# A decoder step on one core: the MLP's second product in seven quarter products for eight

## The chip, the cores and the metric

The kernel runs on one core of a Trainium2 chip. The metric is the device time of one execution in microseconds (us). Three runs of the kernel before took 3097.52, 3102.01 and 3103.74 us; their median, 3102.01 us, is the time that the change is measured against.

## The reference, cut to what matters

One step of a decoder layer on 2048 prompt tokens and 32 sample tokens, in float32. A state-space mixer and a retention mixer come first, then an output projection, an attention over 256 memory tokens, a squared-ReLU MLP and a last normalisation. What the change touches is the MLP:

```
h = rmsnorm(x, p['g_mlp'])                                   # 1024 wide
x = x + jnp.square(jax.nn.relu(h @ p['w_up'])) @ p['w_down']  # 1024 -> 4096 -> 1024
```

## The kernel before

Everything is kept transposed: features on the 128 partitions, tokens along the free axis. A float32 matrix is split into two parts in a 32-bit format that TensorE multiplies fast (float32r): a high part, written by ScalarE as a copy, and a low part, the difference of the number and its high part, written by VectorE (DVE) or GpSimd (POOL). A product is then three passes, high by high, high by low and low by high (PASSES), all summed in one PSUM bank. `mm` (line 445 in the profile) issues each matrix instruction; each loads its own 128 by 128 weight tile (PEld) and streams the tokens past it (PE). All instructions of DVE, ScalarE (ACT), POOL and of the DMA queue on SyncE (SP) go through one helper, line 197, so they are told apart by the names of their tiles.

The tokens are cut into four blocks of 512 columns, numbered 1 to 4 here (0 to 3 in the code). After both mixers have run for all blocks, `rest_items` takes block after block through memory attention and MLP. The sample tokens come into the attention queries with block 2, have their own attention over caches during block 2's MLP (`sample_items`, 48 weight units put between the others, their sums held in one PSUM bank, `zps`), and go through the MLP with block 3, which therefore has 544 columns, taken as two pieces of 272.

Weights come in units of 128 by 1024 numbers (512 KB). `load_unit` (line 413) issues one DMA into `raw` (three buffers), `split_unit` (line 423) makes `whl` of it (high and low part, three buffers): the high part by an ACT copy, the low part by a subtraction on DVE or POOL. Two units are split ahead of the one in use, two more are loaded ahead.

The MLP (`mlp_items`, line 2102) works in eight groups g of 512 hidden features. `up_items(g)` takes four units of `w_up`; each gives one hidden tile of 128 features in 24 matmuls of 512 columns. Each tile then takes a scaled ReLU on DVE from PSUM (`relu`), a square on ACT as high part (`actl`), a square on DVE or POOL (`sq`) and the subtraction of both as low part (`actl`, eight buffers). `down_items(g)` (line 2135) takes four units of `w_down`; each serves two of the eight output tiles, by four hidden tiles, by three passes: again 24 matmuls of 512 columns. At the end of each output tile DVE adds the PSUM bank to the residual `x` (`add_to`, "x<-dn,x"). Order: up(0), up(1), down(0), up(2), down(1), and so on; "dn" in the names of a down matmul is the PSUM tile from `dense` (four banks in turn), "actl" its moving operand. In block 4 the last group's down product runs over the first 256 columns and then over the other 256, and the final normalisation (`final`, line 2186) of the first half starts while the second half is still being multiplied:

```
parts = [(0, BT // 2), (BT // 2, BT)] if g == 7 and B["last"] else [(0, t)]
```

The order of the program is made while it is built. `Order.run` emits the units one after the other, in the order of TensorE's time; chains (`Side`) such as normalisations are resumed when a small model of the engines' rates says that their operands are ready (`poll`). `Either` (line 201) gives an instruction to DVE or to POOL, whichever the model has done with it first, where its key in SET is 2; a weight unit whose engine is None is placed in the same way. Each engine then works through its own instructions strictly in that order.

Of the kernel before, what the change touches and what calls it, by code (L numbers as in the profile page):

```python
# [39 lines left out]
PASSES = ((0, 0), (0, 1), (1, 0))  # L40
GAMMA = [1.0 - 2.0 ** (-5.0 - h) for h in range(HEADS)]
# [16 lines left out]


class Item:  # L60
    """A piece of the main sequence: a weight unit to load and what to do with it, or a call."""
# [13 lines left out]
class Model:  # L75
    """Guesses when each engine does what it is given, from the operands and the engines' rates."""
# [11 lines left out]
    def where(self, ap):  # L88
        """First and last partition and element, outermost stride, elements within it."""
# [93 lines left out]
class Engine:  # L183
    """An engine whose instructions the model sees."""
# [16 lines left out]
class Either:  # L201
    """An instruction for the engine that SET names, or for the one that the model has done with it first."""
# [28 lines left out]
class Order:  # L231
    """Emits the program in the order of the tensor engine's time: a main sequence of weight units,
    and chains that come in between when their latencies have passed."""
# [5 lines left out]
    def spawn(self, gen, *aps):  # L239
        """A chain, from when the tiles are ready."""  # L240
        s = Side(gen, max(self.clock, self.model.ready(*aps)))
        self.sides.append(s)
        return s

    def resume(self, s):
        """A chain goes on when the engines have done what it gave them, or some time later, or when tiles are ready."""
# [15 lines left out]
    def work(self, out, ins, cost):  # L262
        """A matrix product."""
        self.clock = max(self.clock, self.model.after("PE", [out], ins)) + cost
        self.model.note("PE", [out], ins, self.clock)
# [63 lines left out]
def tile_decoder_step(ctx: ExitStack, tc: tile.TileContext, ins: dict, outs: dict):  # L329
# [56 lines left out]
    wo_d = dram.tile([HEADS, 2, P, 1024], F32, tag="wo_d", name="wo_d")  # L386

# [25 lines left out]
    def load_unit(src, into=None):  # L413
        raw = into() if into else wpool.tile([P, 1024], F32, tag="raw", name="raw", bufs=3)
        if isinstance(src, (list, tuple)):
# [7 lines left out]
    def split_unit(raw, eng, pool=None, tag="whl", bufs=NW):  # L423
        """Both float32r parts of a unit, [P, 2, 1024]."""
# [10 lines left out]
    def mm(out, lhsT, rhs, start, stop):  # L435
# [9 lines left out]
        T.matmul(out, lhsT, rhs, start=start, stop=stop)  # L445
# [15 lines left out]
    def split(dst, src, scale=None):  # L461
        """dst[:, 0] + dst[:, 1] = src (* scale) in float32r parts."""
# [3 lines left out]
    def rsqrt(pool, tag, x, n):  # L466
        """x ** -0.5 on [P, n]."""
# [15 lines left out]
    def fm(w, acts, t, out, nk=KT, order=None):  # L483
        """One 128-row tile of W^T X: w(k, s) gives lhsT; fills out with (PSUM tile, column, columns)."""
# [10 lines left out]
    def stats(pool, acc, cols, eps_tag):  # L495
        """(mean square + eps) ** -0.5 by token; cols: list of (lhsT slice of acc, rows, further summands)."""
# [21 lines left out]
    def spread(dst, rs, t, last=None, row=None):  # L518
        """dst[p, token] = rs[token]: rs column i holds tokens i*128.., `last` the sample column; row: space for 512 tokens."""
# [24 lines left out]
    def s5_setup(sp):  # L544
        """The tables and matrices of the state space, four pairs of groups at a time, into DRAM."""
# [27 lines left out]
        def turns(*gens):  # L573
            """One instruction of each in turn."""
# [9 lines left out]
        def poly(x, cs, out):  # L584
            """((cs[0] x + cs[1]) x + ...) x, without a constant term."""
# [123 lines left out]
        # a = mag (cos + i sin), and the parts of a product with it  # L709
# [63 lines left out]
        def products(out, n, x, y, tab, neg):  # L773
            """out gets the real and imaginary parts of (x + i y) tab, the latter with neg for tab."""
# [52 lines left out]
    def all_tables(jt, fhf, fl, hpi):  # L827
        """cos and sin of the angles' multiples."""
# [23 lines left out]
    # The sample tokens go with block SB up to the queries, then through the MLP with the next one.  # L852
# [23 lines left out]
    def fill(side, lst, n):  # L876
        """Runs a chain until lst has n entries."""
        while len(lst) < n and not side.done:
            od.resume(side)

    def fm_item(src, view, acts, t, done, nk=KT, eng=None, order=None, tag="lo"):
        """One weight unit: view(hl) gives a list of w(k, s); done(i, out) takes the i-th result."""
# [54 lines left out]
    def mem_items():  # L937
        """Keys and values of the memory, and the query and output weights with them multiplied in."""
# [105 lines left out]
    def mix_take(B, k, x, rest=None):  # L1044
        """One row tile of the input: its parts and squares; `rest` comes in between."""
# [54 lines left out]
    def first_load(B, units, side):  # L1100
        """The first block's input with the weights of its first product, and a chain in between."""
# [425 lines left out]
    def ret_keep(B, h, i, x):  # L1527
        """Sets the sample columns of a query, key or gate tile aside."""
# [172 lines left out]
    def squares(B, o, t, lo=0):  # L1701
# [10 lines left out]
        else:  # L1712
            sq = rk((P, TM_), "relu", 2) if "rest" in pool else xin()
            A.activation(sq[:, c], x[:, c], AF.Square)
            E("x_rq").tensor_tensor(out=B["acc"][:, c], in0=B["acc"][:, c], in1=sq[:, c], op=ALU.add)
# [11 lines left out]
    def normed_split(B, o, gain, hs, t):  # L1727
        """Its first part; gives what does the second."""
# [161 lines left out]
    def sample_keep(B):  # L1890
        """Sets the sample columns of the normalised input aside."""
# [7 lines left out]
    def sample_items():  # L1899
        """The sample tokens' queries, their attention over the caches, and its output weights."""  # L1900
# [48 lines left out]
    def sample_rows(Z):  # L1949
        """The sum of both parts of the rows in PSUM, and its transpose, tile by tile."""  # L1950
# [93 lines left out]
    def mo_last(B, u, ahead):  # L2044
        """The last two heads, row tile by row tile."""
# [56 lines left out]
    def mlp_items(B, nxt):  # L2102
# [58 lines left out]
        def mixed(items):  # L2161
            for i in items:
                yield i
# [209 lines left out]
```

## Time and profile before

| | |
|---|---|
| median of three runs | 3102.01 us |
| span of the profiled execution | 3086.3 us |
| PE busy | 2950.1 us, 96% |
| DVE, POOL, ACT busy | 1826.7, 1189.3, 1005.9 us |
| mean granted TensorE clock | 0.987 |
| moved by DMA | 374.32 MB |

The profiled execution spans 3086.3 us from its first to its last instruction; the median of the three timed runs lies 15.7 us above that. A duration in the profile is that of one instruction; matrix instructions overlap, so that their pace is read from when they start, not from how long one takes. "[0.85 <-ACT whl L197]" behind a row says that the engine was idle for 0.85 us before it and what ended the idle time. A granted clock of 1.00 is the higher of TensorE's two levels (2.4 GHz).

### The profile page before, as it was taken

How to read it: one execution, taken by the hardware profiler on the slowest of the kernel's cores; microseconds unless marked ns; L12 is line 12 of the kernel's file. 1: busy time of each engine (PE TensorE's matmuls, PEld its weight loads, DVE VectorE, ACT ScalarE, POOL GpSimd, SP SyncE). 2: the span in 40 equal slices, each digit the busy share in tenths (PEclk: the TensorE clock that was granted, in tenths of full speed). 3: DMA queues.
4: the chain of work that ended last, by engine and by line, in shares of the span. 5: the costliest groups of instructions: out<-in, count | busy, mean ns of one | idle time of the engine just before them, and what ended most of it. 6: DMA issues, size and time to landing. Idle time of an engine off the chain costs nothing.

```text
span 3086.3 us, 42360 instructions
## 1 busy us (share of the span) xinstructions
PE 2950.1 (96%) x16676; PEld 2566.3 (83%) x16676; DVE 1826.7 (59%) x3079; ACT 1005.9 (33%) x1440; POOL 1189.3 (39%) x764
## 2 busy tenths in 40 slices
PE   8898899998989999999999999999999999999998
PEld 6788787877877878887987888788999998878887
DVE  9968868679686563334465555655533344554334
ACT  4432232322444332223343333343322223332222
POOL 5424434244454243333524333361523325153333
PEclk9999999999999999999999999999999999999999
DMA  5452252342674322224324444542222233222222
GB/s 150 136 176 97 97 166 96 130 145 72 220 251 157 105 89 96 96 96 140 117 83 138 142 146 147 190 145 89 83 89 89 86 133 119 89 89 96 96 96 75
DMA packets 138950, 374.32 MB, mean 121 GB/s; under 512 B 18656, under 2 KB 39808, under 8 KB 138752
## 3 DMA queue, kind: packets, MB, share of 16 engines
q1 hardware_dynamic: 138176, 371.10, 36.1%
q8 instruction: 131, 2.15, 0.3%
q14 instruction: 67, 0.55, 0.1%
q10 hardware_dynamic: 576, 0.52, 0.1%
HBM read 334.17 MB, written 37.40 MB: 120 GB/s over the span
## 4 chain that ended last, share of the span: by engine, by line
PE 61%; DVE 2%; issue 1%; DMA 1%; ACT 1%; POOL 1%; SPq 0%; POOLq 0%; ACTq 0%; DVEq 0%
PE dn L445 54%; PE sc L445 6%; PE zps L445 1%; DMA raw<-in_w_down 1%; DVE rst L197 1%; ACT whl L197 0%; PE ptp L449 0%; DVE rsy L197 0%; DVE act L197 0%; DVE pmk L197 0%; PE st L445 0%; DVE whl L197 0%; POOL whl L197 0%; POOL act L197 0%; PE sp L445 0%
## 5 line engine op out<-in xcount | busy, mean ns | idle before, releaser
L445 PE MATMUL dn<-act,whl 128*128 128x512 f32 (+2 forms) x4704 | 914.2, 348 | 8.4 <-DVE whl L197 7.4
L445 PE MATMUL dn<-actl,whl 128*128 128x512 f32 (+2 forms) x4656 | 917.3, 356 | 5.1 <-DVE x L197 4.9
L445 PEld LDWEIGHTS dn<-actl,whl 128*128 128x128 f32 x4656 | 767.5, 188 | 134.6 <-issue 3.8
L445 PEld LDWEIGHTS dn<-act,whl 128*128 128x128 f32 x4704 | 753.4, 190 | 116.5 <-DVE whl L197 8.4
L197 POOL TENSOR_TENSOR whl<-raw,whl 128x1024 fp32r<-128x1024 f32 x225 | 559.1, 2487 | 549.1 <-ACT whl L197 536.1
L197 ACT ACTIVATE whl<-raw 128x1024 fp32r<-128x1024 f32 (+1 forms) x505 | 522.7, 1045 | 655.5 <-PE dn L445 445.2
L197 DVE TENSOR_TENSOR x<-dn,x 128x512 f32<-128x512 f32 (+2 forms) x496 | 291.1, 605 | 429.0 <-PE dn L445 428.3
L197 DVE TENSOR_TENSOR whl<-raw,whl 128x1024 fp32r<-128x1024 f32 (+1 forms) x280 | 401.7, 1441 | 165.2 <-ACT whl L197 152.9
L445 PE MATMUL dn<-z,whl 128*128 128x512 f32 (+1 forms) x2160 | 434.9, 353 | 0.0
L445 PEld LDWEIGHTS dn<-z,whl 128*128 128x128 f32 x2160 | 353.7, 188 | 56.8 <-issue 1.1
L197 POOL TENSOR_TENSOR actl<-sq,actl 128x512 fp32r<-128x512 f32 (+1 forms) x128 | 171.3, 1339 | 485.8 <-DVE sq L197 471.5
L197 DVE SCALAR_TENSOR_TENSOR relu<-dn,rb 128x512 f32<-128x512 f32 (+1 forms) x160 | 91.6, 589 | 324.7 <-PE dn L445 317.3
L197 ACT ACTIVATE actl<-relu 128x512 fp32r<-128x512 f32 (+1 forms) x128 | 82.0, 641 | 515.9 <-DVE relu L197 515.9
L445 PE MATMUL dn<-whl,act 128*128 128x512 f32 x768 | 200.1, 408 | 10.8 <-ACT whl L197 6.1
L197 POOL TENSOR_TENSOR acc<-acc,relu 128x512 f32<-128x512 f32 (+2 forms) x77 | 107.4, 1395 | 249.9 <-ACT relu L197 247.8
L445 PEld LDWEIGHTS dn<-whl,act 128*128 128x128 f32 x768 | 165.8, 253 | 34.4 <-ACT whl L197 6.8
L197 DVE TENSOR_TENSOR sq<-relu 128x512 f32<-128x512 f32 (+1 forms) x128 | 90.2, 704 | 14.8 <-POOL actl L197 2.3
L445 PE MATMUL sc<-whl,act 128*128 128x256 f32 x576 | 81.0, 293 | 15.0 <-ACT p L197 9.2
L445 PEld LDWEIGHTS sc<-whl,act 128*128 128x128 f32 x576 | 76.0, 200 | 16.1 <-ACT p L197 9.9
L197 DVE SCALAR_TENSOR_TENSOR act<-x,small,act 128x512 fp32r<-128x512 f32 (+2 forms) x76 | 70.0, 928 | 27.0 <-ACT act L197 26.9
L445 PE MATMUL sc<-whl,z 128*128 128x256 f32 x576 | 80.7, 291 | 0.0
L197 ACT ACTIVATE act<-x,small 128x512 fp32r<-128x512 f32 (+2 forms) x76 | 52.9, 699 | 78.9 <-DVE x L197 55.0
(317 smaller groups left out, 2743.9 us busy)
## 6 DMA issues: line engine op xcount, KB each, us to landing
raw<-in_w_up SPq DMA_DIRECT2D x128, 512.0 KB, 3.5
raw<-in_w_down SPq DMA_DIRECT2D x128, 512.0 KB, 3.5
raw<-in_w_out SPq DMA_DIRECT2D x32, 512.0 KB, 3.5
raw<-wq_d SPq DMA_DIRECT2D x32, 512.0 KB, 3.6
raw<-wo_d SPq DMA_DIRECT2D x32, 512.0 KB, 3.5
x<-in_xT SPq DMA_DIRECT2D x48, 256.0 KB, 4.3
pm<-pm_d SPq DMA_DIRECT2D x16, 768.0 KB, 4.6
tab<-tab_d SPq DMA_DIRECT2D x16, 516.0 KB, 3.5
```

Of the source, the lines that this page charges most:

```text
L197: return f(*args, **kw)
L445: T.matmul(out, lhsT, rhs, start=start, stop=stop)
```

## The change

In blocks 2 to 4 the down product of each group is done by Strassen's scheme in the form with few additions. For each group and each half u of the output tiles, the weights are seen as a 2 by 2 matrix of quarters, each 256 hidden features by 256 outputs, and the hidden tiles as a 2 by 2 matrix of quarters, each 256 features by half of the block's tokens. Seven products of quarters (JOBS) stand for eight; each has 12 matmuls of 256 columns (272 in block 3).

- The hidden squares are written to `hc` by DVE or POOL. A chain `hidden(g)` makes the four sums of them, and the two float32r parts of all seven operands: 4 subtractions, 7 ACT copies and 7 more subtractions, each on 2 by 256 columns. It goes on only as far as buffers of `actl` have been read.
- The sums of the weights' quarters, S1 to S4, don't depend on the block. `sums()` makes them while the first block is in its attention and MLP: 32 times a DMA of 512 KB in, four POOL subtractions or additions of 256 columns, a DMA of 512 KB out to `s_d`.
- `down_seven` pairs the 14 products of a group into seven weight units. A unit's halves come from the weights in a new layout (`w_s`) or from `s_d`, in one DMA, or in two of half the size when they don't lie beside each other.
- Partial sums stay in PSUM where they are needed again: A11, S2, S3 and A22 are added up in one bank, S1 and S4 in another, A12 has its own. After each product DVE adds the bank as it stands to the residual, two tiles of 256 columns, 28 such additions per group.
- In block 4 the last group isn't cut into halves of the columns any more, and the final normalisation runs once, over all 512 columns, behind the last product.
- `dynamic_dma_scratch_size` is made smaller.

```diff
+HQ = TM_ // 2
+JOBS = ("A11", "A12", "S2", "S1", "S3", "S4", "A22")
...
+    "l_ds": 4, "x_hs": 2, "x_hq": 2, "x_hl": 2, "q_h": 250, "ws": 700, "ws1": 1500, "ws2": 5000}
...
+    s_d = dram.tile([16, P, 4, 512], F32, tag="s_d", name="s_d")
...
+        src = src() if callable(src) else src
...
-            E("x_rq").tensor_tensor(out=B["acc"][:, c], in0=B["acc"][:, c], in1=sq[:, c], op=ALU.add)
+            (V if "tail" in B else E("x_rq")).tensor_tensor(out=B["acc"][:, c], in0=B["acc"][:, c], in1=sq[:, c], op=ALU.add)
...
-        def mixed(items):
-            for i in items:
+        def hidden(g, c):
+            h, ops = t // 2, a_of[g]
+            b11, b12, b21, b22 = (c[:, :, i, :h] for i in range(4))
+            def sub(out, a, b):
+                E("x_hs").tensor_tensor(out=out, in0=a, in1=b, op=ALU.subtract)
+            def keep(name, src):
+                before = divmod(7 * g + JOBS.index(name) - NL, 7)
+                while g and B["prog"] < 14 * before[0] + 8 + before[1]:
+                    yield 300
+                yield [src]
+                a = actl().rearrange("p a (s c) -> p a s c", s=2)
+                A.activation(a[:, :, 0, :h], src, AF.Copy)
+                yield [a]
+                E("x_hl").tensor_tensor(out=a[:, :, 1, :h], in0=src, in1=a[:, :, 0, :h].bitcast(F32), op=ALU.subtract)
+                ops[name] = a
+                yield SET["q_h"]
+            yield [c]
+            t2 = rk((P, 2, HQ), "t2")[:, :, :h]
+            yield from keep("A11", b11)
+            sub(b11, b12, b11)
+            sub(t2, b22, b11)
+            yield from keep("A12", b21)
+            sub(b21, b21, t2)
+            yield from keep("S2", t2)
+            sub(b12, b22, b12)
+            yield from keep("S1", b11)
+            yield from keep("S3", b12)
+            yield from keep("S4", b22)
+            yield from keep("A22", b21)
+        def up_seven(g):
+            a_of[g] = {}
+            c_of = {}
+            for m in range(4):
+                def done(_, out, m=m):
+                    def ev():
+                        if m == 0:
+                            c_of[0] = rk((P, 2, 4, HQ), "hc")
+                        c = c_of[0]
+                        r = rk((P, TM_), "relu", 2)
+                        for ps, lo, n in out:
+                            V.scalar_tensor_tensor(out=r[:, lo:lo + n], in0=ps[:, :n], scalar=0.0,
+                                                   in1=B["mrb"][:, lo:lo + n], op0=ALU.max, op1=ALU.mult)
+                        v = r[:, :t].rearrange("p (a b) -> p a b", a=2)
+                        E("x_hq").tensor_tensor(out=c[:, m // 2, 2 * (m % 2):2 * (m % 2) + 2, :t // 2], in0=v, in1=v, op=ALU.mult)
+                        if m == 3:
+                            hid[g] = od.spawn(hidden(g, c))
+                    if m == 0 and g:
+                        while not hid[g - 1].done:
+                            od.resume(hid[g - 1])
+                    ev() if "mrb" in B else pend.append(ev)
+                yield fm_item(ins["w_up"][4 * g + m], one, lambda: B["hm"], t, done, eng=ve("e_up1" if m % 2 else "e_up"), tag="l_up")
+        def seven(g, u, name, st):
+            h = t // 2
+            def job(w):
+                v = w.rearrange("p s (k m c) -> p s k m c", k=2, m=2)
+                while name not in a_of[g]:
+                    od.resume(hid[g])
+                for m in range(2):
+                    if name in ("A11", "S1"):
+                        st[name, m] = (aux2 if name == "S1" and not held["zps"] else dense)("m7")
+                    ps = st["S1" if name in ("S1", "S4") else "A11", m] if name != "A12" else aux("m7")
+                    for k in range(2):
+                        for i, (a, b) in enumerate(PASSES):
+                            mm(ps[:, :h], v[:, a, k, m, :], a_of[g][name][:, k, b, :h],
+                               start=(name in ("A11", "A12", "S1") and k + i == 0), stop=(k == 1 and i == 2), skip_group_check=True)
+                        yield
+                    o = 4 * u + m + (2 if name in ("A22", "S1", "S3") else 0)
+                    lo = h if name in ("S2", "S4", "S1", "S3") else 0
+                    V.tensor_tensor(out=B["x"][o][:, lo:lo + h], in0=ps[:, :h], in1=B["x"][o][:, lo:lo + h], op=ALU.add)
+                    if name == "A22" and g == 7:
+                        if B["last"] and u:
+                            B["tail"] = True
+                        squares(B, o - 2, t)
+                        squares(B, o, t)
+                B["prog"] = 14 * g + 7 * u + JOBS.index(name) + 1
+            return job
+        def down_seven(g):
+            jobs = []
+            for u in range(2):
+                st = {}
+                for name in JOBS:
+                    src = {"A11": ("w", 0), "A22": ("w", 1), "A12": ("w", 3), "S2": ("s", 0), "S1": ("s", 1),
+                           "S3": ("s", 2), "S4": ("s", 3)}[name]
+                    jobs.append((seven(g, u, name, st), src + (2 * g + u,)))
+            for a, b in zip(jobs[0::2], jobs[1::2]):
+                def fn(hl, a=a, b=b):
+                    for i, j in enumerate((a, b)):
+                        yield from j[0](hl[:, :, 512 * i:512 * i + 512])
+                yield Item(fn, seven_src(a[1], b[1]), tag="l_ds")
+            if g == 7:
+                yield call(lambda: B.__setitem__("fin", od.spawn(final(B, 0, t), B["acc"])))
+        def mixed(items, part=1.0):
+            for n, i in enumerate(items):
                 yield i
+                if i.src is not None and int((n + 1) * part) == int(n * part):
+                    continue
                 if B["sample"]:
                     for _ in range(WHEN.count(count[0])):
                         yield from next(smp)
@@ -2168,20 +2275,55 @@
         count, smp = [0], sample_items()
         yield call(lambda: B.__setitem__("ms", od.spawn(mlp_scale(), B["acc"])))
-        yield from up_items(0)
+        hid = {}
+        B["prog"] = 0
+        use = [B["b"] > 0] * 8
+        yield from (up_seven if use[0] else up_items)(0)
         yield Item(None, side=lambda: B["ms"])
         for g in range(8):
             if g < 7:
-                yield from mixed(up_items(g + 1))
+                yield from mixed((up_seven if use[g + 1] else up_items)(g + 1))
             if g == 6 and nxt is not None:
                 def pre():
                     nxt["cl"] = od.spawn(cat_load(nxt))
                     x_load(nxt, range(NX - KT))
                 yield call(pre)
-            yield from mixed(down_items(g))
+            yield from mixed(down_seven(g), 4.0 / 7.0 + 1e-6) if use[g] else mixed(down_items(g))
         if B["sample"]:
             for x in smp:
                 yield from x
+    summed = set()
+    def sums():
+        for n in range(16):
+            for h in (slice(0, 256), slice(256, 512)):
+                q = rk((P, 4, 256), "wsum")
+                SY.dma_start(q, ins["w_s"][n][:, :, h])
+                yield [q]
+                yield SET["ws1"]
+                for out, a, b, op in ((1, 1, 2, ALU.add), (2, 0, 2, ALU.subtract), (0, 1, 0, ALU.subtract),
+                                      (3, 3, 0, ALU.subtract)):
+                    G.tensor_tensor(out=q[:, out], in0=q[:, a], in1=q[:, b], op=op)
+                    yield SET["ws"]
+                yield [q]
+                yield SET["ws1"]
+                SY.dma_start(s_d[n][:, :, h], q)
+                yield SET["ws2"]
+            summed.add(n)
+    def seven_src(a, b):
+        def src(x):
+            while x[0] == "s" and x[2] not in summed:
+                od.resume(M["sums"])
+            return (ins["w_s"] if x[0] == "w" else s_d)[x[2]]
+        def get():
+            if a[0] == b[0] and a[2] == b[2]:
+                return [src(a)[:, a[1]:b[1] + 1:b[1] - a[1]]]
+            return [src(x)[:, x[1]].rearrange("p (a b) -> p a b", a=1) for x in (a, b)]
+        return get
...
+        yield call(lambda: M.__setitem__("sums", od.spawn(sums())))
...
+    dn = a["w_down"][0].reshape(8, 2, 2, P, 2, 2, 2, P).transpose(0, 4, 5, 2, 3, 1, 6, 7).reshape(16, 2, 2, P, 512)
+    out["w_s"] = c(np.stack([dn[:, 0, 0], dn[:, 1, 1], dn[:, 1, 0], dn[:, 0, 1]], 2))
...
-    nc = _bacc.Bacc("TRN2", target_bir_lowering=False, num_devices=1)
+    nc = _bacc.Bacc("TRN2", target_bir_lowering=False, num_devices=1, dynamic_dma_scratch_size=1024)
```

## Rows read from the trace of the kernel before

**Rows 1.** The page: busy time by engine, and the chain of waits by line.
```profile
PE 2950.1 (96%) x16676; PEld 2566.3 (83%) x16676; DVE 1826.7 (59%) x3079; ACT 1005.9 (33%) x1440; POOL 1189.3 (39%) x764
...
PE dn L445 54%; PE sc L445 6%; PE zps L445 1%; DMA raw<-in_w_down 1%; DVE rst L197 1%; ACT whl L197 0%; PE ptp L449 0%; DVE rsy L197 0%; DVE act L197 0%; DVE pmk L197 0%; PE st L445 0%; DVE whl L197 0%; POOL whl L197 0%; POOL act L197 0%; PE sp L445 0%
```

**Rows 2.** PE's waits, 2226 to 3020 us: us in total, times, longest.
```profile
PE dn L445 <- DVE x L197: 3.4, 2, 3.0
...
```

**Rows 3.** Windows: length, busy PE, PEld, DVE, ACT, POOL (instructions), clock, DMA share, GB/s.
```profile
1286.00:1308.40 22.40, 22.40 (x97) 18.03 (x96) 9.02 (x11) 4.76 (x5) 6.09 (x3) 1.00 0.35 118
...
1667.91:1694.20 26.29, 26.29 (x118) 20.40 (x117) 13.51 (x16) 10.10 (x12) 11.73 (x8) 1.00 0.51 175
...
2226.52:2250.60 24.08, 24.08 (x194) 24.08 (x193) 9.91 (x19) 4.79 (x5) 6.17 (x3) 1.00 0.32 110
...
2806.57:2828.54 21.97, 21.97 (x98) 17.99 (x96) 9.03 (x11) 4.77 (x5) 6.10 (x3) 1.00 0.34 120
2828.54:2850.69 22.15, 22.15 (x97) 18.02 (x96) 8.19 (x9) 5.81 (x7) 8.66 (x5) 1.00 0.22 72
```

**Rows 4.** Timeline of PE at the end: start, us, instructions, idle before.
```profile
3049.18 2.96 PE L445 MATMUL dn<-actl,kv 128*128 128x256 f32 x24
...
3060.46 2.98 PE L445 MATMUL dn<-actl,kv 128*128 128x256 f32 x24
...
3069.74 3.07 PE L445 MATMUL dn<-actl,whl 128*128 128x256 f32 x24
3073.75 0.35 PE L445 MATMUL st<-ones,acc 128*128 128x2 f32 x2 [0.94 <-DVE acc L197]
```

**Rows 5.** Groups by form, 2806.57 to 2828.54 us: busy, mean ns | idle before.
```profile
L445 PEld LDWEIGHTS dn<-actl,whl 128*128 128x128 f32 x95 | 17.8, 187 | 3.9
L197 DVE TENSOR_TENSOR x<-dn,x 128x512 f32<-128x512 f32 x7 | 4.8, 690 | 9.5 <-PE dn L445 9.5
L197 POOL TENSOR_TENSOR whl<-raw,whl 128x1024 fp32r<-128x1024 f32 x2 | 4.8, 2406 | 6.8 <-ACT whl L197 6.8
L197 ACT ACTIVATE whl<-raw 128x1024 fp32r<-128x1024 f32 x4 | 4.2, 1057 | 12.0 <-PE dn L445 8.8 <-issue 3.2
...
L197 POOL TENSOR_TENSOR actl<-sq,actl 128x512 fp32r<-128x512 f32 x1 | 1.3, 1292 | 1.9 <-DVE sq L197 1.9
L197 DVE TENSOR_TENSOR sq<-relu 128x512 f32<-128x512 f32 x1 | 0.7, 693 | 0.1
...
L197 ACT ACTIVATE actl<-relu 128x512 fp32r<-128x512 f32 x1 | 0.6, 634 | 4.0 <-DVE relu L197 4.0
```

**Rows 6.** Timeline of DVE in the last half product: two instructions in a row.
```profile
3065.82 0.42 DVE L197 TENSOR_TENSOR x<-dn,x 128x256 f32<-128x256 f32 x1
3066.15 0.41 DVE L197 TENSOR_TENSOR acc<-acc,relu 128x256 f32<-128x256 f32 x1
```

**Rows 7.** Timeline: the same DVE split without POOL at work, and with it.
```profile
2824.34 1.23 DVE L197 TENSOR_TENSOR whl<-raw,whl 128x1024 fp32r<-128x1024 f32 x1 [0.40 <-ACT whl L197]
...
2835.90 1.30 POOL L197 TENSOR_TENSOR actl<-sq,actl 128x512 fp32r<-128x512 f32 x1 [3.57 <-DVE sq L197]
2836.60 1.68 DVE L197 TENSOR_TENSOR whl<-raw,whl 128x1024 fp32r<-128x1024 f32 x1 [0.85 <-ACT whl L197]
```

**Rows 8.** Timeline behind block 2's attention: a DVE split between two POOL instructions.
```profile
1618.21 3.32 POOL L197 TENSOR_TENSOR acc<-acc,relu 128x512 f32<-128x512 f32 x2
...
1620.31 2.31 DVE L197 TENSOR_TENSOR whl<-raw,whl 128x1024 fp32r<-128x1024 f32 x1
```

**Rows 9.** The tile `raw`, 2760 to 3020 us: count, min/median/max.
```profile
L197 DVE TENSOR_TENSOR whl<-raw,whl x24: 1226/1666/1679, 2765.0 to 3018.7; 128x1024 fp32r<-128x1024 f32 x24
...
DMA to landing us min/median/max: 3.3/3.5/4.0
```

More of the change, by code (lines that the diff above doesn't have):

```diff
@@ L433, in tile_decoder_step, with mm @@
     od = Order(model, load_unit, split_unit)
-    def mm(out, lhsT, rhs, start, stop):
+    def mm(out, lhsT, rhs, start, stop, **kw):
         n = 1
@@ L444, in mm @@
         od.work(out, [lhsT, rhs], c)
-        T.matmul(out, lhsT, rhs, start=start, stop=stop)
+        T.matmul(out, lhsT, rhs, start=start, stop=stop, **kw)
     def tr(out, in_, idn):
```

2 rows, old and new, of the table SET are left out of this document.

## The prediction

> **What bounds the kernel now.** I read the page first: PE is busy for 96% of the span, and in the chain of waits by line the matmuls into the banks "dn" alone hold 54% [rows 1]. Then PE's waits: in the 794 us of blocks 3 and 4 its matmuls into "dn" waited 3.4 us for DVE's additions, in two places [rows 2]. Then the windows, one for each up or down phase of a group. PE is busy for the whole of each: 22.40 us for a down phase in block 1, 24.08 in block 3 (544 columns), 21.97 in block 4, and the up phases take as long (22.15). DVE works 9.0 of a down phase's 22.0 us, POOL 6.1, ACT 4.8, and the clock is at its higher level [rows 3]. So the down product is bound by PE's pace, with the helpers half idle. Fewer matmul columns there are time saved, as long as the helpers still keep up.
>
> The sum is made against the profiled execution, whose span of 3086.3 us is 15.7 us under the median of the runs. I take differences from it and apply them to 3102.0.
>
> **The matmuls.** Before, a group's down phase has 96 matmuls of 512 columns; after, 2 halves by 7 products by 12 = 168 of 256. The kernel before has that form already, with its own weight tile for each matmul, in block 4's last group: from the start at 3049.18 to that at 3060.46 lie 96 matmuls of 256 columns, 11.28 / 96 = 0.1175 us each [rows 4]. A down phase is then 168 x 0.1175 = 19.74 us. Block 2: 8 x (22.40 - 19.74) = 21.3 us, with block 1's phase as the price, since block 2's own holds sample units. Block 4: 7 x (21.97 - 19.74) = 15.6, and its last group, which is now 192 matmuls of 256 columns (22.6 us), saves 24 of them, 2.8: 18.4. Block 3 has 272 columns before and after, so one eighth goes: 8 x 24.08 / 8 = 24.1. Together 63.8 us. The up phases keep their matmuls.
>
> A weight load lasts 187 ns on its row [rows 5], longer than the 117.5 ns from one matmul to the next, so loads run beside matmuls. The Trainium skill ("TensorE: Matmul & The Clock Gate", The mechanism) says that loads overlap running matmuls only where their row groups differ; full 128-row tiles share theirs, and halving the columns would then double a cost that is not hidden. This trace contradicts it: 0.1175 us for load and matmul together [rows 4]. By the rule the change would lose hundreds of us; by the row it gains 63.8.
>
> **The end.** The last product ended about 3072.8 (chain of 24 from 3069.74, 3.07 us long) [rows 4], and the span at 3086.3: 13.5 us. Now all 512 columns come behind it. Squares, sums and the eight scaled tiles are twice as wide: a 512-column addition takes 690 ns where one of 256 takes 420 [rows 5, 6], on POOL 1292 ns. With some ten such instructions in a row on the path, that adds 10 x 0.27 = 2.7 us, and the longer way of spreading the row scale about another 1: 4 us, bounds 2 and 7.
>
> **The helpers.** In a down phase of 19.7 us DVE has 28 additions of 256 columns. One lasts 0.42 us, but the next instruction starts 0.33 us after it [rows 6]: 28 x 0.33 = 9.2 us. There are seven units to split in place of four: seven ACT copies of 1.06 us and seven subtractions, 1.23 us on DVE [rows 7] or 2.41 on POOL [rows 5]. Beside them come the 11 subtractions of the hidden chain (693 ns on DVE, 1292 on POOL) and its seven ACT copies of 634 ns [rows 5]. ACT has 7 x 1.06 + 7 x 0.63 = 11.8 of 19.7 us and is no bound. All the rest on DVE would be 9.2 + 8.6 + 7.6 = 25.4 us. That is over 19.7, so the planner has to move 5.7 us of it to POOL: 2 splits and 5 subtractions (2.46 + 3.47 = 5.9) become 4.8 + 6.5 = 11.3 us there. By the engines' own times this fits, at 99% of DVE.
>
> But the two engines are not independent. A DVE split takes 1.23 us alone and 1.68 when it starts while POOL's subtraction still has 0.60 us to go [rows 7]; between two POOL instructions it took 2.31 [rows 8]; half of block 4's 24 DVE splits took 1.67 or more [rows 9]. So such a split is held by a running POOL instruction, for 0.45 to 1.08 us, and the additions queue behind it. There is leeway: a bank is multiplied into again three half products later, 3 x 0.705 = 2.1 us. Split, usual hold and addition are 1.23 + 0.45 + 0.42 = 2.1: just used up. One hidden subtraction more in the queue (0.69), or a longer hold, and PE waits. With seven POOL instructions in a phase the price per phase is between nothing (leeway and idle time of the up phase take all) and 4 us (seven holds of 1.08, half of which reach PE). I take 1.3, three usual holds, because the row of 0.45 is the frequent one: 24 x 1.3 = 31 us, bounds 0 and 96.
>
> **Supply of weights.** A unit is now used up in 24 x 0.1175 = 2.82 us. A raw buffer is taken for 3.5 us of DMA [rows 9], 1.06 of ACT and 1.23 to 2.41 of subtraction, 0.45 more when held: 6.2 to 7.4 us, by three buffers 2.1 to 2.5 us per unit. It fits with 0.3 us to spare: nothing in blocks 3 and 4, and 0.3 x 112 units = 34 us if halved DMAs land a microsecond later. In block 2 the sample units (DVE 13.5 of 26.3 us already, DMA share 0.51 [rows 3]) come between, and the sample's bank takes one that S1 uses elsewhere. All four "dn" banks are then taken, and the next half's first product waits for the last addition but one, with only one half product (0.7 us) of leeway. I take 4 us, bounds 0 and 15.
>
> **Sums in block 1.** 128 POOL instructions of about 0.7 us (1292 ns for 512 columns [rows 5]) and 32 MB of DMA lie beside PE, where POOL had 6 of 22 us [rows 3]; what remains are holds of DVE in front of the attention's short chains: 1 us, bounds 0 and 6. The smaller scratch costs nothing, as no DMA here is made by POOL.
>
> **Sum.** 63.8 - 31 - 4 - 4 - 1 = 24 us less; I round the gain down to 23: 3102 - 23 = 3079 us. About a third of the matmuls' gain is left.
>
> **Rivals.**
> - *Helpers hidden.* The planner's order keeps POOL's instructions out of the way of the splits. For it: the idle time in up phases, where DVE works 8.2 of 22.2 us [rows 3]; the chain of g has a whole group's time. Against: its gates put ten of its subtractions in the second half of the down phase. Price 0.2 us per phase: 63.8 - 5 - 4 - 3 - 1 = 51, 3051 us.
> - *All eaten.* Holds of 2.2 us per phase: 63.8 - 53 - 9 = 2; 3100 us, no change that can be told (under 0.2%, 6.2 us, a measurement of this kernel can't tell one).
> - *DVE becomes the bound (slower).* In the down phase's second half 3.5 splits, eight hidden subtractions and 14 additions meet in 9.9 us. If each split or subtraction on DVE waits for POOL's current instruction, half of 1292 ns on average, five such waits are 3.2 us, and DVE's queue has no slack to take them. At 3.5 us per phase: 63.8 - 84 - 12 = -32; 3134 us. It decides from 2.3 us per phase on. For it: [rows 7, 8]. Against: in the rows most holds were 0.45 us. The Trainium skill ("GPSIMD Engine Reference", 1. Specifications) states that GpSimd's memory interface is shared with DVE instructions that have two SBUF inputs. By that rule all splits and hidden subtractions contend and the PSUM additions don't, which is this rival's mechanism; the rows agree.
> - *Weight loads exposed*, so that the smaller products don't do what they are to: each matmul 0.187 + 0.1175 us, a phase 51 us, 24 phases over 690 us more: 3790 us. [Rows 4] speak against it.
>
> **How the numbers follow.** Forecast (3063 to 3096) 0.35, helpers hidden 0.24, all eaten 0.14, DVE the bound 0.25, loads exposed 0.02. Faster by over 0.2%: 0.35 + 0.24 = 0.59; same 0.14; slower 0.27. Range: 3043 to 3124, which leaves out some 0.08 below (no holds at all and a short end) and 0.12 above. The forecast's own range is 3063 to 3096.
>
> **What would show it.** Matmuls of 256 columns into "m7" or "dn" at 0.1175 us from start to start; down phases of about 21 us in block 4 (19.8 if the helpers are hidden, 23 and more if DVE is the bound); PE's waits headed by DVE's additions "x<-", more in the second half of a phase; DVE splits with a median over 1.67 us; the end 17 to 18 us behind the last product. I am wrong if PE waits for weights more than for additions, if the pace of the matmuls is not 0.1175, or if block 1 grows by more than 6 us.

## The result: 6.3% slower

The changed kernel took 3295.27 us (median of five runs, 3290.76 to 3358.52), the kernel before 3102.01 us; the ratio is 1.0632 (95% interval 1.0603 to 1.066). In a second series it was 3285.47 to 3095.29, a ratio of 1.0624 (1.0594 to 1.0653). One of the first five executions, the profiled one, had a lower granted clock (0.863 in the mean, 3358.52 us), so it isn't in the ratio, and what follows is read from the second series' profile of the same kernel, span 3278.6 us.

The page of the profile: busy time by engine, against [rows 1], and the chain by line.

```profile
PE 2976.2 (91%) x17530; PEld 2633.0 (80%) x17530; DVE 2258.2 (69%) x3690; ACT 1121.8 (34%) x1570; POOL 1393.0 (42%) x909
...
PE dn L450 15%; PE m L450 7%; DVE hc L200 2%; PE sc L450 2%; DVE whl L200 2%; DVE x L200 1%; DVE t L200 1%; POOL hc L200 0%; DVE actl L200 0%; DVE rst L200 0%; POOL actl L200 0%; POOL acc L200 0%; DMA x<-cat_d 0%; PE ptp L454 0%; DVE rsy L200 0%
```

DVE is busy for 431 us more, and PE, which had next to no gaps in the down phases of blocks 3 and 4, now has them. PE's waits say for whom: the matmuls into the quarter products' banks ("m") wait for DVE's additions. The rows are for the whole span, for the down phases of blocks 3 and 4 without the last two of block 4 (2299 to 3205 us; over that stretch [rows 2] had 3.4 us in all), and for one down phase (2952.41 to 2981.50 us).

```profile
PE m L450 <- DVE x L200: 142.8, 68, 4.9
PE m L450 <- DVE x L200: 98.0, 44, 4.9
PE m L450 <- DVE x L200: 6.4, 5, 3.2
```

Windows of the changed kernel, columns as in [rows 3]: a down and an up phase of block 3; in block 4 the down phases of groups 0 and 1, with the up phase behind the latter; last the MLPs of blocks 2, 3 and 4, from the first matmul of up(0) to the first matmul of the next block (in block 4 to the end).

```profile
2299.12:2332.82 33.70, 25.10 (x170) 24.47 (x169) 28.79 (x39) 11.48 (x14) 14.93 (x7) 0.85 0.30 95
2332.82:2356.95 24.13, 24.13 (x195) 24.13 (x193) 9.57 (x16) 4.25 (x4) 2.39 (x1) 1.00 0.36 109
2900.12:2930.24 30.12, 23.65 (x169) 22.66 (x168) 24.66 (x36) 11.28 (x14) 17.31 (x8) 0.89 0.37 116
2952.41:2981.50 29.09, 22.66 (x170) 21.68 (x168) 24.61 (x36) 11.29 (x14) 17.36 (x8) 0.94 0.38 117
2981.50:3003.66 22.16, 22.16 (x98) 18.03 (x97) 11.89 (x14) 4.25 (x4) 2.40 (x1) 1.00 0.34 110
...
1620.47:2099.31 478.84, 420.41 (x2475) 365.06 (x2473) 363.23 (x499) 191.35 (x241) 205.50 (x114) 0.94 0.50 157
2244.84:2702.69 457.85, 394.04 (x2896) 388.60 (x2894) 316.04 (x455) 137.03 (x166) 151.11 (x73) 0.92 0.35 109
2847.60:3278.60 431.00, 366.79 (x2133) 323.91 (x2131) 301.91 (x431) 132.49 (x160) 166.12 (x78) 0.94 0.34 108
```

The same three MLPs before:

```profile
1616.58:2028.86 412.28, 408.46 (x1899) 327.80 (x1898) 238.06 (x280) 153.42 (x195) 166.83 (x97) 1.00 0.45 152
2175.06:2569.73 394.67, 390.30 (x3087) 389.23 (x3086) 165.14 (x281) 98.24 (x119) 133.78 (x73) 1.00 0.28 96
2715.06:3086.30 371.24, 358.73 (x1663) 296.43 (x1661) 154.27 (x214) 96.50 (x126) 137.58 (x83) 0.99 0.27 91
```

They lose 66.6, 63.2 and 59.8 us, together 189.5 of the 192.3 us between the two spans. The up phases inside blocks 3 and 4 keep their time; the down phases go from 22 to 29 us in block 4 and from 24.1 to 33.7 in block 3. In the phase from 2952.41 PE is busy for 22.66 of 29.09 us: 6.4 us of waiting, all of it for DVE's additions, and a busy time above the 19.7 us that the prediction gives its matmuls.

That phase on the timeline, from its start:

```profile
2952.41 5.83 PE L450 MATMUL m<-actl,whl 128*128 128x256 f32 x48
...
2954.61 2.03 DVE L200 TENSOR_TENSOR whl<-raw,whl 128x1024 fp32r<-128x1024 f32 x1
...
2956.57 0.41 DVE L200 TENSOR_TENSOR x<-m,x 128x256 f32<-128x256 f32 x1
...
2957.78 5.14 POOL L200 TENSOR_TENSOR whl<-raw,whl 128x1024 fp32r<-128x1024 f32 x2
2957.85 2.82 DVE L200 TENSOR_TENSOR t<-hc 128x512 f32<-128x512 f32 x1 [0.87 <-POOL hc L200]
...
2960.59 2.29 DVE L200 TENSOR_TENSOR x<-m,x 128x256 f32<-128x256 f32 x6
2961.48 11.69 PE L450 MATMUL m<-actl,whl 128*128 128x256 f32 x84 [3.24 <-DVE x L200]
...
2964.76 0.42 DVE L200 TENSOR_TENSOR x<-m,x 128x256 f32<-128x256 f32 x1 [0.86 <-PE m L450]
2966.04 0.42 DVE L200 TENSOR_TENSOR x<-m,x 128x256 f32<-128x256 f32 x1 [0.86 <-PE m L450]
2966.83 0.42 DVE L200 TENSOR_TENSOR x<-m,x 128x256 f32<-128x256 f32 x1 [0.37 <-PE m L450]
2967.54 0.42 DVE L200 TENSOR_TENSOR x<-m,x 128x256 f32<-128x256 f32 x1 [0.28 <-PE m L450]
...
2970.71 2.31 DVE L200 TENSOR_TENSOR whl<-raw,whl 128x1024 fp32r<-128x1024 f32 x1
...
2973.28 1.43 DVE L200 TENSOR_TENSOR hc<-hc,t 128x512 f32<-128x512 f32 x1
2973.41 0.98 PE L450 MATMUL m<-actl,whl 128*128 128x256 f32 x6 [0.24 <-DVE x L200]
...
2974.97 2.52 DVE L200 TENSOR_TENSOR hc<-hc 128x512 f32<-128x512 f32 x1
...
2978.41 1.88 DVE L200 TENSOR_TENSOR actl<-hc,actl 128x512 fp32r<-128x512 f32 x1
```

DVE's subtraction `t<-hc` takes 0.69 us where POOL has no work (the row is with the run "everything on DVE" below). Here DVE first waited 0.87 us for POOL's result; then POOL began a split 0.07 us ahead of it, and the subtraction takes 2.82. An instruction that lasts longer because the other engine is at work is called held here. Six additions stand behind this one in DVE's queue, and PE waits 3.24 us for the third product's bank. Then PE works, but for a time at the lower of its two levels: the additions follow the half products, and those at 2964.76 and 2966.04 are 1.28 us apart, 6 matmuls of 0.213; a little later they are 0.71 us apart again (2966.83 to 2967.54). The clock column says the same, 0.50 and then 1.00:

```profile
2963.00:2966.00 3.00, 3.00 (x16) 3.00 (x15) 0.85 (x2) 0.00 (x0) 0.00 (x0) 0.50 0.70 213
2966.10:2973.10 7.00, 7.00 (x60) 6.87 (x59) 6.07 (x10) 4.36 (x6) 2.44 (x2) 1.00 0.23 78
```

Four more held instructions follow before the phase ends.

### The profile page after: what moved, and what is told of

It is laid out like the page before. It is cut to its first block, busy times and chain, and to the rows that moved or that the text cites. A ratio compares the mean times of both kernels' runs of the same rounds, so it can differ in the third digit from the quotient of the medians.

```text
span 3356.7 us, 45558 instructions
## 1 busy us (share of the span) xinstructions
PE 3092.8 (92%) x17530; PEld 2686.1 (80%) x17530; DVE 2253.4 (67%) x3690; ACT 1123.1 (33%) x1570; POOL 1390.1 (41%) x909
## 5 line engine op out<-in xcount | busy, mean ns | idle before, releaser
L450 PE MATMUL m<-actl,whl 128*128 128x256 f32 (+1 forms) x4032 | 568.8, 303 | 148.9 <-DVE x L200 140.3
L450 PEld LDWEIGHTS m<-actl,whl 128*128 128x128 f32 x4032 | 546.4, 207 | 171.4 <-issue 67.8
L450 PE MATMUL dn<-actl,whl 128*128 128x512 f32 x1536 | 383.9, 412 | 0.0
L450 PEld LDWEIGHTS dn<-actl,whl 128*128 128x128 f32 x1536 | 292.1, 191 | 82.9 <-DVE whl L200 0.5
L200 POOL TENSOR_TENSOR actl<-hc,actl 128x512 fp32r<-128x512 f32 (+1 forms) x60 | 89.0, 1487 | 557.6 <-ACT actl L200 538.5
L200 DVE TENSOR_TENSOR x<-m,x 128x256 f32<-128x256 f32 (+1 forms) x672 | 260.5, 420 | 66.4 <-PE m L450 64.9
L200 DVE TENSOR_TENSOR x<-dn,x 128x512 f32<-128x512 f32 (+1 forms) x232 | 152.5, 670 | 205.2 <-PE dn L450 204.6
L200 POOL TENSOR_TENSOR acc<-acc,relu 128x512 f32<-128x512 f32 (+1 forms) x73 | 108.6, 1488 | 213.1 <-ACT relu L200 208.5
L200 POOL TENSOR_TENSOR wsum<-wsum 128x256 f32<-128x256 f32 x128 | 117.8, 920 | 70.5 <-DMA wsum<-in_w_s 65.1
L200 DVE TENSOR_TENSOR actl<-hc,actl 128x512 fp32r<-128x512 f32 (+1 forms) x84 | 92.1, 1110 | 1.1 <-ACT actl L200 0.8
```

Of the source, the lines that this page charges most:

```text
L200: return f(*args, **kw)
L450: T.matmul(out, lhsT, rhs, start=start, stop=stop, **kw)
```

## Experiments

Two theories were put against each other: *held queue* (DVE's instructions with two inputs in SBUF, the on-chip memory beside PSUM, stand behind POOL's, and the additions behind them) and *DVE full* (it has more to do than the phase lasts).

**The kernel again** (no edit).

> The changed kernel itself once more, for a second profile of it. Two theories are to be told apart by the runs beside it. Held queue: DVE's instructions with two SBUF inputs stand behind POOL's, DVE works in order, so the additions behind them come late and PE waits for its banks; after a long wait PE's clock falls. DVE full: DVE has simply more to do in a down phase than it lasts, holds or none. Both expect 3295 us (3285 to 3305), down phases of block 4 of about 29 us, PE idle 6 of them, PE's waits headed by DVE's additions, over 100 us in all.

Measured: as above; both theories fit the total and the waits. The timeline already speaks against *DVE full*: six instructions of the phase are held, for 7.8 us together, so that of DVE's 24.6 us 16.8 are work of its own.

**Everything on DVE.**

```diff
-    "l_ds": 4, "x_hs": 2, "x_hq": 2, "x_hl": 2, ...
+    "l_ds": 4, "x_hs": 0, "x_hq": 0, "x_hl": 0, ...
-   ... t, done, eng=ve("e_up1" if m % 2 else "e_up"), tag="l_up")   # in up_seven
+   ... t, done, eng=V, tag="l_up")
-                yield Item(fn, seven_src(a[1], b[1]), tag="l_ds")
+                yield Item(fn, seven_src(a[1], b[1]), V, tag="l_ds")
```

> In the groups with seven products all splits of weights, all hidden squares and subtractions are put on DVE, so that POOL has nothing there. Held queue: DVE has more to do, 33 us per group of some 42, but is never held; down phases fall from 29 to 22 to 25 us, 3120 to 3190 us in all. DVE full: the 11 us per phase that POOL did come on top for DVE; down phases of 33 us or more, 3390 us or more.

Measured: 3149.74 us, ratio 1.0177 (1.016 to 1.0193). DVE got POOL's work on top of its own and the kernel became 136 us faster. A down phase of block 4, then the subtraction `t<-hc` (min/median/max) in this run:

```profile
2861.23:2883.95 22.72, 21.36 (x169) 20.21 (x168) 22.09 (x43) 11.08 (x14) 0.00 (x0) 1.00 0.43 133
...
L200 DVE TENSOR_TENSOR t<-hc x6: 691/691/693, 2821.3 to 3045.8; 128x512 f32<-128x512 f32 x6
```

and the same subtraction in the changed kernel:

```profile
L200 DVE TENSOR_TENSOR t<-hc x7: 2821/2824/2824, 2905.6 to 3215.1; 128x512 f32<-128x512 f32 x7
```

*DVE full* falls as the cause of 29 us. It returns at a lower level: at 22.09 of 22.72 us DVE is now the bound, and 22.7 is not under the 22.0 of before. What the whole kernel still loses lies for the most part in block 2, whose MLP takes 453.1 us for 412.3 before.

**Everything on POOL** (the same places with 1 and G; hidden squares on DVE).

> In the groups with seven products all splits of weights and all hidden subtractions are put on POOL (the hidden squares on DVE). DVE has only additions from PSUM, the scaled ReLU and the squares. Held queue: PE's waits for DVE's additions nearly go (under 10 us in all); POOL has 11 x 2.41 + 11 x 1.29 = 40.7 us per group and now nearly sets the pace; waits for POOL's operands or weights in their place; 3060 to 3170 us. DVE full: the same, as DVE is unloaded; a third theory, that the banks come back too soon for any addition (three half products later), expects waits for DVE's additions as before, over 100 us.

Measured: 3241.15 us, ratio 1.0474 (1.0447 to 1.0502); the waits for DVE's additions fell to 19.6 us, so the third theory (banks come back too soon) falls, but the total was expected lower. In block 4 the forecast held: POOL sets the pace, 40.04 us of the 44.77 of a down and an up phase.

```profile
2953.52:2975.02 21.50, 20.13 (x169) 19.92 (x168) 12.87 (x30) 8.99 (x10) 19.25 (x11) 1.00 0.47 141
2975.02:2998.29 23.27, 22.42 (x99) 17.96 (x97) 10.63 (x7) 6.44 (x8) 20.79 (x12) 1.00 0.37 120
```

Most of the rest is block 2, whose MLP takes 513.6 us and where PE waited 51.8 us for POOL's splits.

**Sums only.**

```diff
-        use = [B["b"] > 0] * 8
+        use = [False] * 8
```

> The weights' sums are made in the first block as in the change, but all blocks take the old down product, so that the sums are read by nobody. Both theories: the sums cost little, 3102 us plus 0 to 10. A rival, that a good part of the loss comes from the sums (POOL's work and 32 MB of DMA beside the first block): 3140 us or more.

Measured: 3098.18 us, ratio 1.0013 (0.9996 to 1.003). The sums, and the smaller scratch with them, cost between nothing and 9 us.

**Work on POOL that nobody waits for**, added to "everything on DVE":

```diff
+            B["junk"] = rk((P, 4, 256), "wsum").rearrange("p a b -> p (a b)")   # per block, when the sums are done; zeroed by POOL
...
                 def fn(hl, a=a, b=b):
+                    G.tensor_tensor(out=B["junk"], in0=B["junk"], in1=B["junk"], op=ALU.subtract)
```

> The kernel with everything on DVE (3150 us), and in each of its seven units per down phase one POOL subtraction of 128x1024 on a tile that nobody reads: 2.4 us each, 17 of some 23 us. Nothing waits for its result. Held queue: DVE's splits and subtractions stand behind it again, the additions behind them, down phases of block 4 go from 22.6 to 26 to 32 us, 3230 to 3370 us in all, and the granted clock falls in these phases. DVE full: no change, 3150 us (within 10).

Measured: 3338.98 us, ratio 1.0774 (1.0755 to 1.0792), 189 us above the run without it, which was timed in another series (ratio 1.0177). In one thing the expectation was wrong: POOL, waiting for nothing, ran through its instructions ahead of time, in one go. That made a comparison inside one block, the first down phase of block 4 with POOL at work and the second without:

```profile
2986.17:3029.85 43.68, 26.82 (x170) 25.19 (x168) 42.56 (x44) 11.17 (x14) 42.35 (x18) 0.77 0.30 91
3052.01:3074.76 22.75, 21.37 (x169) 20.24 (x168) 22.14 (x43) 11.08 (x14) 0.00 (x0) 1.00 0.47 133
```

DVE does the same work in both (44 and 43 instructions); with POOL busy it is "busy" for 42.6 us, as long as POOL. No result of POOL is waited for here, so waits for operands from POOL can't be the cause.

**POOL's splits alone beside the hidden chain on DVE:** down splits on POOL, up splits and hidden subtractions on DVE (as above with 0, V and G), and the squares on ACT:

```diff
-   E("x_hq").tensor_tensor(out=c[:, m // 2, ...], in0=v, in1=v, op=ALU.mult)
+   A.activation(c[:, m // 2, ...], v, AF.Square)
```

> Down splits all on POOL, up splits and the hidden subtractions on DVE, hidden squares on ACT; the hidden chain stays in the down phase. DVE's own work in a down phase is then only 28 additions and some eight subtractions, 14 of 20 us. Held queue: the hidden subtractions still stand behind POOL's splits of 2.4 us, so that PE waits: down phases 22 to 26 us, 3090 to 3190 us. DVE full: no waits, down phases 20 us, 3050 to 3075 us.

Measured: 3284.54 us, ratio 1.0591 (1.0568 to 1.0613), as slow as the change and slower than expected. DVE's groups by form in a down phase of block 4 (28.90 us):

```profile
L200 DVE TENSOR_TENSOR x<-m,x 128x256 f32<-128x256 f32 x26 | 10.4, 418 | 5.3 <-PE m L450 5.3
L200 DVE TENSOR_TENSOR actl<-hc,actl 128x512 fp32r<-128x512 f32 x4 | 5.3, 1313 | 0.0
L200 DVE TENSOR_TENSOR hc<-hc 128x512 f32<-128x512 f32 x2 | 3.2, 1602 | 0.0
L200 DVE TENSOR_TENSOR t<-hc 128x512 f32<-128x512 f32 x1 | 2.7, 2710 | 0.0
```

Seven subtractions of 0.69 us take 1.3 to 2.7 in the mean of their groups; the additions, one input of which lies in PSUM, keep their 0.42. The seven are held for 6.3 us in all, not much less than the 7.8 of the changed kernel, and PE waits 5.8 us. DVE's own work would be 17.0 of its 23.3 us, well under the phase, so *DVE full* doesn't explain this run either.

**The hidden chain in the up phase,** on top of that:

```diff
+            while 0 < g < 7 and B["prog"] < 14 * g:    # first lines of hidden(g, c)
+                yield 300
```

> As the run beside it, but for groups 0 to 6 the hidden chain waits until the down phase before has been issued, and so runs in the up phase, where DVE adds nothing from PSUM but four ReLUs. In a down phase DVE has then only additions, none of which POOL can hold, and POOL 7 splits, 17 of 20 us. Held queue: down phases of 19.8 to 20.5 us, up phases as before (22), 3040 to 3080 us: faster than both kernels. Banks come back too soon (third theory): waits for additions stay, 3130 us or more. Weights too slow from POOL: waits for POOL's splits, 3090 to 3130.

Measured: 3165.22 us, ratio 1.0216 (1.0199 to 1.0234): the phases came as expected, the total didn't. A down phase of block 3 and one of block 4:

```profile
2312.58:2333.64 21.06, 21.06 (x170) 21.06 (x169) 14.06 (x30) 7.99 (x8) 11.90 (x5) 1.00 0.56 165
2885.14:2905.16 20.02, 20.02 (x170) 19.93 (x168) 13.76 (x29) 7.95 (x8) 11.94 (x5) 1.00 0.54 159
```

PE has no gap left in them; in block 4 the other phases of this kind take 19.87 us. What is lost lies in block 2 (481.3 us for 412.3), and in the last two down phases, which follow each other and hold group 7's chain (65.86 us in block 3, 58.24 in block 4).

**Old product in block 2, and the last groups' down splits on DVE.** In the first of two runs only group 6's splits went to DVE (`V if g == 6 else G`), in the second group 7's too:

```diff
-        use = [B["b"] > 0] * 8
+        use = [B["b"] > 1] * 8
-                yield Item(fn, seven_src(a[1], b[1]), G, tag="l_ds")
+                yield Item(fn, seven_src(a[1], b[1]), V if g >= 6 else G, tag="l_ds")
```

> The run with the hidden chain in the up phase, with two more edits: block 2, with the sample's units, keeps the old product; and in group 6's down phase, the only one that still has a hidden chain in it (group 7's), the splits go to DVE, so that POOL has nothing there. Held queue: block 3 loses 13 us of its last two phases and block 4 too (65.8 to some 52.5, 58.2 to some 45.2), down phases of 20.9 and 19.75 us, 3065 to 3092 us in all, faster than both kernels. Against it, that something else eats what the matmuls gain: 3095 us or more.

> The run before it with the splits of the last group's down phase on DVE as well. There the splits on POOL still held the end of group 7's hidden chain: 65.1 us in block 3 and 50.3 in block 4 for the last two down phases, where the kernel with all on DVE took 52.6 and 45.2. Held queue: about these 52.6 and 45.2, so 18 us less than the run before it, 3065 to 3078 us. If the two phases are bound by DVE's own work or by the next block's loads there: no change, 3083 to 3093 us.

Measured: 3087.93 us, ratio 0.997 (0.9958 to 0.9982), and 3076.61 us, ratio 0.9923 (0.9907 to 0.9939). Both are faster than both kernels, by 0.3% and 0.8% against the kernel before. The last two down phases of block 4 in the first and the second:

```profile
3015.99:3066.40 50.41, 43.92 (x337) 43.04 (x335) 37.02 (x73) 19.73 (x25) 21.33 (x10) 0.93 0.35 104
```

```profile
3015.73:3061.24 45.51, 41.64 (x337) 40.10 (x335) 41.38 (x80) 19.61 (x25) 4.55 (x3) 1.00 0.39 115
```

In block 3 they hardly fell in the first run (65.15 us, where some 52.5 were expected), and take 55.96 in the second, where 52.6 were expected; both totals stayed within the expectation. In the second run's profile the MLPs of blocks 3 and 4 take 378.1 and 362.7 us, 16.5 and 8.6 less than before.

**Block 2 without POOL:** the sample's units behind the MLP's, everything on DVE; in the second run S1 and S4 take the "dn" banks all the same.

```diff
-                if B["sample"]:                       # in mixed
-                    for _ in range(WHEN.count(count[0])):
-                        yield from next(smp)
...
+        held["zps"] = held["zps"] or B["sample"]      # the second run alone
```

> The kernel with everything on DVE, with the sample's 48 units of block 2 not put between the MLP's units but all behind them, so that the sample's bank is taken only then. What block 2 loses without POOL (47 us) is to be split. If it is the sample's work between the units (its splits on DVE, its loads): block 2's down phases are 22.6 us as in block 4. The total says nothing, as the sample's units then stand alone.

> The run beside it, but S1 and S4 take the four dn banks in block 2 all the same, as they do where the sample's bank is held. If the banks are the cause, each change from one half of the outputs to the other waits for the last additions: block 2's down phases 24 to 28 us. If they are not: 22.6 to 23.

Measured: 3203.5 and 3210.5 us, and a down phase of block 2 lasts the same in both, from its start to that of the up phase behind it:

```profile
1712.09:1734.82 22.73, 21.37 (x170) 20.23 (x169) 22.10 (x43) 11.08 (x14) 0.00 (x0) 1.00 0.43 132
```

```profile
1715.45:1738.18 22.73, 21.36 (x169) 20.22 (x168) 22.09 (x43) 11.07 (x14) 0.00 (x0) 1.00 0.45 133
```

By themselves the banks cost nothing that is seen; what they cost with the sample's units between wasn't tried. With the units between, the first six down phases of block 2 take 25.8 to 32.1 us in the run with everything on DVE, 29.0 in the mean: 6.3 more than without. Before, they took 25.5 to 26.3, in the mean 3.6 more than block 1's 22.40 [rows 3], with PE busy throughout, so that much of the 6.3 is the units' own products. The other large part of block 2's loss is its last two down phases. The shortest and the longest of the six and the last two, with everything on DVE, and then the last two before:

```profile
1850.76:1876.55 25.79, 24.07 (x197) 23.12 (x195) 25.62 (x48) 13.90 (x19) 0.00 (x0) 1.00 0.54 166
1739.11:1771.24 32.13, 25.83 (x196) 24.66 (x195) 29.82 (x53) 15.36 (x22) 6.19 (x6) 0.95 0.48 150
2012.96:2083.26 70.30, 56.32 (x369) 51.45 (x368) 56.17 (x94) 31.99 (x43) 9.99 (x7) 0.85 0.61 196
```

```profile
1976.48:2028.86 52.38, 51.16 (x225) 39.70 (x224) 34.82 (x34) 25.27 (x33) 31.01 (x16) 1.00 0.63 217
```

How much of all this is the units' splits on DVE, how much their loads, and how much POOL's remaining work (38.54 us in that MLP) stays open.

## Why the prediction was wrong

- *What bounds the kernel* and *the matmuls*: right. Without gaps the 168 matmuls of a down phase take 19.87 to 20.02 us in block 4, up to the next phase's first matmul (19.74 forecast), and 21.06 in block 3 (21.07 forecast). Weight loads are hidden.
- *The helpers*: the step that failed, by the size of its term. The mechanism stood there, and again as the slower rival with its price of 3.5 us per phase; I gave that 0.25 and put 1.3 us into the sum, three holds of 0.45, because that row was "the frequent one". In the changed kernel a phase of block 4 lasts 29.09 us, 9.1 more than without gaps, one of block 3 33.70, 12.6 more. The holds of the phase from 2952.41 are 7.8 us: each of DVE's six held instructions took 0.7 to 2.1 us longer than alone (2.03 and 2.31 for 1.22 of a split; 2.82, 2.52, 1.88 and 1.43 for 0.69). [Rows 7] showed a hold by a POOL subtraction that was more than half over. In the new phase the two engines get their work at the same moment, and a POOL split of 2.4 us holds a DVE instruction for nearly all of its length. The bound of 4 us had the holds nearly right (seven of 1.08, 7.6 us) and failed where it let half of them reach PE: PE waited 6.4 us.
- A cost that was in no term: PE's pace after a wait. The phase in block 4 has 22.66 us of PE for 20.02 of work, that in block 3 25.10 for 21.06, at granted clocks of 0.94 and 0.85; without gaps the same phases run at 1.00. So of the 9.1 us in block 4 some 6.4 are waiting and 2.6 are longer busy time; of the 12.6 in block 3, 8.6 and 4.0. Of the 2.6, about 1.6 are the lower clock: the 84 matmuls from 2961.48 take 11.69 us, where 84 x 0.1175 is 9.87, and 0.27 more for the end of the last. The rest are such ends: six matmuls before a wait fill 0.98 us where six starts take 0.71.
- *Block 2*: 4 us taken, bounds 0 and 15, off a gain of 21.3. The MLP of the block loses 66.6 us, and 40.8 (453.1 for 412.3) even with all on DVE. The reason given, a bank short, showed no cost where it was tried alone. What the runs show in its place is the holds, the sample's units and the last two down phases; how the latter come about stays open.
- *Supply of weights*: right for blocks 3 and 4: the phases without gaps use up seven units in 20 us, and from 2299 to 3205 us of the changed kernel no wait of the "m" matmuls is put down to weights.
- *The end*: right, 17 to 18 us forecast. PE's timeline of the changed kernel ends the products at 3261.2, and the span is 3278.6: 17.4 us, 4 more than before.

```profile
3256.68 4.52 PE L450 MATMUL m<-actl,whl 128*128 128x256 f32 x36 [1.28 <-DVE x L200]
```

- *Sums*: 1 us taken, bounds 0 and 6; the measured interval, 0 to 9, fits. Block 1, from its first matmul to block 2's, took 524.4 us in the changed kernel's profile and 526.0 before.
- *What would show it* named signs that came, those of the slower rival: phases of "23 and more if DVE is the bound", PE's waits headed by additions.

## What to carry to other kernels

Before work is moved to DVE and POOL, count which of DVE's instructions read two tensors from SBUF: those and POOL's took turns here, and a short one stood behind POOL's longest. If DVE also frees PSUM banks, keep POOL's instructions out of the stretches in which it has such instructions to do; here moving them to another phase made the same arithmetic, on the same engines as in the run before it, go without a gap in all but the last two down phases of blocks 3 and 4. A slack worked out from a row of a calm stretch isn't the slack of a dense one: price a hold by the longest instruction that can stand in front, and add what PE's clock then loses.

## What the hardware showed that was not expected

- DVE's instructions on two SBUF tensors and POOL's shut each other out for whole instructions, both ways: a DVE subtraction of 0.69 us took 2.82 behind a POOL split, and POOL's own subtraction on `hc`, behind a DVE split, 2.17 us in place of 1.29. In the changed kernel's block 4 (min/median/max):

```profile
L200 POOL TENSOR_TENSOR actl<-hc,actl x14: 1289/1297/1298, 2902.0 to 3227.9; 128x512 fp32r<-128x512 f32 x14
L200 POOL TENSOR_TENSOR hc<-hc x7: 2168/2171/2174, 2903.4 to 3212.9; 128x512 f32<-128x512 f32 x7
```

  With POOL at work without a pause, DVE's 22 us of work took 42.6.
- The granted clock fell in stretches in which PE waited some microseconds at a time: 0.94 and 0.85 in phases with 6.4 and 8.6 us of gaps, 0.77 in the phase with 16.9 us of them, 1.00 in the phases without. The sum of the gaps doesn't set it: 0.89 in the phase from 2900.12, with 6.5 us of them. The MLPs of the same blocks had 0.99 to 1.00 before.
